# Forgetting attention of a four-layer network: the rows of log gates spread over the partitions by DMA from DRAM instead of by one-hot matmuls

## The chip, the cores and the metric

One Trainium2 chip, one of its cores. The metric is the device time of the whole kernel in microseconds (us), as the median of its runs; below, times inside the program are those of one profiled execution.

## What is computed

The reference runs two blocks, one after the other. The first has two layers on 512 + 256 tokens (differential attention with a gated delta net, then neighbourhood attention). The second has two "hybrid" layers on 528 tokens, 16 learned ones and 512 others; each has eight heads of forgetting attention, four heads of retention, a projection and a feed-forward part. The change is in the forgetting attention:

```python
def fox_attention(q, k, v, logf):
    # logit[t,s] = q_t.k_s/sqrt(Dh) + c[t] - c[s], c = cumsum(log f), s <= t
...
logf = jax.nn.log_sigmoid(flog.astype(jnp.float32) + b_fgate.astype(jnp.float32))
fox_out = fox_attention(fq.reshape(fshape), fk.reshape(fshape), fv.reshape(fshape), logf)
```

A softmax over s is not altered by c[t], which is the same in a whole row of logits. What the kernel has to add is -c[s]: one row of 528 numbers per head, the same on all partitions, since queries lie on the partitions and keys along the free dimension.

## The kernel before, in words

**Arithmetic.** Every product of weights is taken in exact halves: a weight tile arrives by DMA on SP's queue in one of four raw buffers (`top.wraw`), ACT casts its high half (`top.whi`, L457), DVE takes the low half (`top.wlo`, L458), and TensorE does three matmuls for each pair of tiles (L581 and L862).

**Order.** The program is written through a scheduler of tiles. Each piece of work stands in a stream ("L" for projections, "A" for forgetting attention, "B" for retention) with PSUM banks of its own; `later(n)` gives work a lower place, so that it fills gaps of the stream beside it. The order of each engine, which is fixed when the program is built, comes out of that. SBUF for larger tiles is cut into zones (`NZONE`, 24 of them), which are handed out for the whole program, the longest free first.

**A hybrid layer** (`hybrid`, L2192). The five tiles of the first projection give the raw gates and the queries and keys of pairs 0 and 1. `fox_gates` (L1622) makes the log gates, sums them along the tokens and ends with eight rows of 528, times -8, as exact halves `rh`, `rl` (ACT L1666, DVE L1667). Then come `fox(0)`, `fox(1)`, `ret(0)`, `fox(2)`, `ret(1)`, `fox(3)`, the tail, `ret(2)`, `ret(3)` and the projection out. `fox(p)` does the projections of a pair of heads and puts `fox_pair` (L1715) under `later(200)`, so that its small matmuls stand among those of the retention's projection (`retproj.L`, L581).

**A pair.** For each of its two heads, `fox_pair` takes a ring tile `cb` of 128 x 512, and spreads the head's row over 128 partitions: two matmuls (L1729) of a one-hot column of the 8 x 8 identity, broadcast to 128 columns, by the rows, high half and low half, into a PSUM tile `fox.A`, and an ACT copy (L1730) to `cb`. The ring has two tiles. Then, for query tiles 0 and 1, 2, and 3, come q k products (L1742), the causal mask (L1745), the sum with `cb` and its maximum on DVE (L1754), the exponential on ACT (L1757), transposes (L688 by way of a helper) and the product with the values (L1768).

**The tail.** `fox_tail` (L1671) does the last 16 queries of all heads as one tile of 128 rows, in two halves of 272 and 256 keys. Per half there are q k products (L1681), two matmuls with a constant `hselr` that gives rows 16 h to 16 h + 15 the log gates of head h (L1685), an ACT copy (L1686), in the second half a mask (L1688), and the sum and maximum (L1689).

Of the kernel before, what the change touches and what calls it, by code (L numbers as in the profile page):

```python
# [11 lines left out]
F32 = mybir.dt.float32  # L12
# [8 lines left out]
P = 128  # L21
D = 1024
KT = D // P
T = 512
# [9 lines left out]
NZONE = 24  # L34
# [14 lines left out]
# ---------------------------------------------------------------- host layout  # L49

def _fm(w):
    """[K, N] -> [N/128, 128, K]: per column tile, the K tiles side by side."""
    k, n = w.shape
    return np.ascontiguousarray(
        w.reshape(k // P, P, n // P, P).transpose(2, 1, 0, 3)).reshape(n // P, P, k)


def _tm(w):
    """[1024, N] -> [N/256, 2, 128, 1024]: 256-column chunks in two halves of K."""
# [5 lines left out]
def _col(v):  # L65
    """[..., n*128] -> [128, ... * n] (feature on partitions)."""
# [4 lines left out]
def _rows(v):  # L71
    """1-d data repeated on all partitions."""
# [4 lines left out]
def _down(w, groups):  # L77
    """[2816, 1024] -> flat pieces per (hidden group, output tile)."""
# [10 lines left out]
def _headperm(n_heads, dh):  # L89
    """columns of each dh-wide head: even ones first, then odd ones."""  # L90
# [4 lines left out]
# order of the grid's columns in the neighbourhood layer: rolled by 8 columns, column-major  # L95
# [8 lines left out]
def _na_bias(rpb):  # L104
    """[8, 15, 31] -> [8, 128, 3, 256]: bias of each query tile's two key tiles (first, inner, last)."""
# [14 lines left out]
def _const_tables():  # L120
# [7 lines left out]
    # masks added to logits: causal [query, key], and its mirror  # L128
# [4 lines left out]
    hq = np.arange(P) // META  # L133
    t["hsel"] = np.zeros((P, P), f)
    t["hsel"][:8] = np.arange(8)[:, None] == hq[None]
    t["tmask"] = np.where(np.arange(META)[None] <= (a % META)[:, None], 0.0, NEG).astype(f)
    t["mask1"] = ((blk[:, None] == blk[None] + 1) & (blk[:, None] % 2 == 1)).astype(f)
    # rotary tables of the grid positions, even dims first
# [10 lines left out]
    # rotary tables of the second block  # L149
# [5 lines left out]
    # retention decay: [key, query - first key of the tile], key scale folded in  # L155
# [8 lines left out]
def layout(i):  # L164
# [9 lines left out]
    # [l, section, k, 128, 1024]  # L174
    o["ada_w"] = np.ascontiguousarray(g["ada_w"].reshape(2, KT, P, 6, D).transpose(0, 3, 1, 2, 4))
    # the first two sections, by quarters of the columns: [quarter, half of the features, 128, 4 tiles, 256]
# [50 lines left out]
# ---------------------------------------------------------------- kernel  # L227

class K:
    def __init__(self, tc, a, out, ctx):  # L230
# [11 lines left out]
        self.used = np.zeros((NZONE, ZONE // UNIT))     # when a unit was given back; inf: in use  # L242
# [14 lines left out]
    # ------------------------------------------------------------ SBUF: zones of one type, given out in pieces  # L257
    def take(self, n, dtype=F32, top=False, low=False, ring=False, pack=None):
        """n free columns of a zone of the type, or of an empty one: those that have been free for longest."""
# [2078 lines left out]
```

## Time and profile before

| | |
|---|---|
| runs shown (us) | 3464.41, 3473.41, 3473.85; median 3473.41 |
| span of the profiled execution (us) | 3471.1 |
| median less that span (us) | 2.3 |
| mean granted TensorE clock | 0.983 |
| PE busy | 3331.4 us, 96% |
| DVE, ACT, POOL busy | 65%, 41%, 25% |
| DMA | 101 GB/s, SP's queue (q1) 29.9% of 16 engines |

The span runs from the first to the last instruction; a run's time also takes in what lies around it. PE is TensorE's matmuls and PEld its weight loads, which lie beside them. The views with stretches give busy microseconds of each engine in a stretch, and the clock that TensorE was granted there, as a share of full speed (1.00 is 2.4 GHz, 0.50 is 1.2 GHz).

### The profile page before, as it was taken

How to read it: one execution, taken by the hardware profiler on the slowest of the kernel's cores; microseconds unless marked ns; L12 is line 12 of the kernel's file. 1: busy time of each engine (PE TensorE's matmuls, PEld its weight loads, DVE VectorE, ACT ScalarE, POOL GpSimd, SP SyncE). 2: the span in 40 equal slices, each digit the busy share in tenths (PEclk: the TensorE clock that was granted, in tenths of full speed). 3: DMA queues.
4: the chain of work that ended last, by engine and by line, in shares of the span. 5: the costliest groups of instructions: out<-in, count | busy, mean ns of one | idle time of the engine just before them, and what ended most of it. 6: DMA issues, size and time to landing. Idle time of an engine off the chain costs nothing.

```text
span 3471.1 us, 63453 instructions
## 1 busy us (share of the span) xinstructions
PE 3331.4 (96%) x25746; PEld 3071.4 (88%) x25746; DVE 2243.5 (65%) x4401; ACT 1423.0 (41%) x2617; POOL 862.7 (25%) x708
## 2 busy tenths in 40 slices
PE   7999989999999999999999999999999999999998
PEld 6877867799999899998999988899999988889998
DVE  6566766696885655546967844458688543478766
ACT  4355442353444334335433443334344443334434
POOL 0001152053341102111543410005235100033533
PEclk9999999999999999999999999999999999999999
DMA  6112256323335763112233411121333311123232
GB/s 216 42 36 69 81 165 197 125 92 98 104 109 184 275 234 94 63 44 90 72 94 100 128 65 53 49 73 63 98 104 94 121 41 59 34 92 98 88 102 96
DMA packets 124070, 350.52 MB, mean 101 GB/s; under 512 B 27904, under 2 KB 31104, under 8 KB 123776
## 3 DMA queue, kind: packets, MB, share of 16 engines
q1 hardware_dynamic: 116288, 337.17, 29.9%
q10 hardware_dynamic: 7488, 9.29, 0.9%
q8 instruction: 202, 3.31, 0.4%
q14 instruction: 92, 0.75, 0.1%
HBM read 331.73 MB, written 14.68 MB: 100 GB/s over the span
## 4 chain that ended last, share of the span: by engine, by line
PE 54%; DVE 13%; issue 7%; ACT 3%; POOL 1%; DMA 1%; DVEq 0%; ACTq 0%; POOLq 0%; SPq 0%
PE ffn.L L581 20%; PE ffn.L L862 10%; PE retproj.L L581 5%; PE foxproj.L L581 4%; DVE top.wlo L854 4%; PE naproj.L L645 3%; PE outp.L L581 2%; PE fox.A L1742 2%; DVE top.zone L896 1%; ACT top.whi L853 1%; PE fox.Ao L1768 1%; PE ret.B L1825 1%; PE naattn.Ao L1586 1%; PE fox.A L688 1%; PE ada.E L918 1%
## 5 line engine op out<-in xcount | busy, mean ns | idle before, releaser
L457 ACT CAST top.whi<-top.wraw 128x1024 fp32r<-128x1024 f32 (+2 forms) x305 | 294.4, 969 | 543.2 <-PE ffn.L L581 245.2
L458 DVE TENSOR_TENSOR top.wlo<-top.wraw,top.whi 128x1024 fp32r<-128x1024 f32 (+2 forms) x305 | 353.4, 1162 | 232.4 <-ACT top.whi L457 230.8
L862 PE MATMUL ffn.L<-outp.zone,top.whi 128*128 128x256 f32 (+1 forms) x1862 | 407.5, 282 | 8.5 <-ACT top.whi L853 8.5
L862 PEld LDWEIGHTS ffn.L<-outp.zone,top.whi 128*128 128x128 f32 x1862 | 309.1, 189 | 9.3 <-ACT top.whi L853 9.3
L862 PE MATMUL ffn.L<-outp.zone,top.wlo 128*128 128x256 f32 (+1 forms) x1026 | 292.7, 285 | 16.5 <-DVE top.wlo L854 16.1
L581 PE MATMUL ffn.L<-ffn.zone,top.whi 128*128 128x256 f32 (+1 forms) x1460 | 295.9, 283 | 0.0
L854 DVE TENSOR_TENSOR top.wlo<-top.wraw,top.whi 128x1024 fp32r<-128x1024 f32 x152 | 241.9, 1592 | 52.5 <-ACT top.whi L853 52.0
L581 PE MATMUL ffn.L<-outp.zone,top.whi 128*128 128x256 f32 (+1 forms) x1214 | 272.5, 282 | 0.5 <-ACT top.whi L457 0.4
L862 PE MATMUL ffn.L<-norm.zone,top.whi 128*128 128x256 f32 (+1 forms) x1178 | 265.3, 283 | 0.0
L845 POOL TENSOR_TENSOR top.zone<-top.wraw,top.wraw 128x512 f32<-128x512 f32 x76 | 116.6, 1535 | 594.5 <-DMA top.wraw<-in_w_up_dram 494.1
L581 PEld LDWEIGHTS ffn.L<-ffn.zone,top.whi 128*128 128x128 f32 x1460 | 233.4, 189 | 0.6 <-DVE ffn.zone L899 0.4
L862 PE MATMUL ffn.L<-norm.zone,top.wlo 128*128 128x256 f32 (+1 forms) x798 | 227.6, 285 | 5.9 <-DVE top.wlo L854 5.6
L862 PEld LDWEIGHTS ffn.L<-outp.zone,top.wlo 128*128 128x128 f32 x1026 | 193.8, 189 | 23.2 <-DVE top.wlo L854 23.0
L581 PE MATMUL ffn.L<-ffn.zone,top.wlo 128*128 128x256 f32 (+1 forms) x758 | 213.1, 282 | 0.0
L581 PEld LDWEIGHTS ffn.L<-outp.zone,top.whi 128*128 128x128 f32 x1214 | 203.2, 189 | 2.6 <-issue 1.6
L853 ACT CAST top.whi<-top.wraw 128x1024 fp32r<-128x1024 f32 x152 | 158.8, 1045 | 102.1 <-PE ffn.L L581 69.1
L862 PEld LDWEIGHTS ffn.L<-norm.zone,top.whi 128*128 128x128 f32 x1178 | 199.7, 189 | 0.3 <-ACT top.whi L853 0.2
L581 PE MATMUL ffn.L<-gsolve.zone,top.whi 128*128 128x256 f32 x688 | 164.7, 287 | 0.3 <-ACT top.whi L457 0.3
L862 PEld LDWEIGHTS ffn.L<-norm.zone,top.wlo 128*128 128x128 f32 x798 | 151.1, 189 | 8.6 <-DVE top.wlo L854 8.6
L854 DVE TENSOR_TENSOR top.wlo<-top.zone,top.whi 128x1024 fp32r<-128x1024 f32 x76 | 144.6, 1903 | 8.0 <-ACT top.whi L853 8.0
L581 PE MATMUL ffn.L<-outp.zone,top.wlo 128*128 128x256 f32 (+1 forms) x528 | 148.7, 282 | 0.0
L862 PE MATMUL ffn.L<-gsolve.zone,top.whi 128*128 128x256 f32 (+1 forms) x570 | 146.2, 283 | 0.0
(1369 smaller groups left out, 9959.8 us busy)
## 6 DMA issues: line engine op xcount, KB each, us to landing
top.wraw<-in_w_up_dram SPq DMA_DIRECT2D x220, 512.0 KB, 3.5
top.wraw<-in_w_dn_dram SPq DMA_DIRECT2D x89, 448.0 KB, 3.4
top.wraw<-in_w_hy_dram SPq DMA_DIRECT2D x58, 512.0 KB, 3.5
top.zone<-in_ada_w_dram SPq DMA_DIRECT2D x48, 512.0 KB, 5.4
top.wraw<-in_w_dn_dram SPq DMA_DIRECT2D x40, 512.0 KB, 3.7
top.wraw<-in_ada_w_dram SPq DMA_DIRECT2D x32, 512.0 KB, 5.0
top.wraw<-in_w_gdn_dram SPq DMA_DIRECT2D x17, 512.0 KB, 3.5
quads.zone<-in_ada_w_dram SPq DMA_DIRECT2D x16, 512.0 KB, 4.7
```

The costliest lines, as they stand in the source:

```text
L457: nc.scalar.copy(hi[:, :m], raw[:, c:c + m])
L458: nc.vector.tensor_sub(lo[:, :m], raw[:, c:c + m], hi[:, :m].bitcast(F32))
L581: nc.tensor.matmul(ps[:, :n], w[:, wc], x[ks[j]][:, c0:c0 + n], start=a, stop=b)
L645: nc.tensor.matmul(pst[t][:, :256], cols(x, k, t), ww[:, wc], start=a, stop=b)
L688: self.nc.tensor.transpose(dst[:, i * P:i * P + m], s, self.ident[:m, :m])
L845: nc.gpsimd.tensor_sub(s23[:, 512:], rg[:, :512], ru[:, :512])
L853: nc.scalar.copy(wh[:, :m], src)
L854: nc.vector.tensor_sub(wl[:, :m], src, wh[:, :m].bitcast(F32))
L862: nc.tensor.matmul(ps[:, :h], ww[:, wc], xx[k], start=st, stop=sp)
L896: nc.vector.tensor_mul(sg[:, :n], sg[:, :n], su[:, :n])
L918: nc.tensor.matmul(ps[32 * g:32 * g + 32, :256], self.sil[:, k, :], w[:, g * 256:(g + 1) * 256], start=k == 0, stop=k == KT - 1, tile_posi ...
L1742: nc.tensor.matmul(ss[r][:, off[i] + a:off[i] + b], fq[fs, i * P:n], fk[fs, a:b], start=True, stop=b < n)
```

## The change

The rows are kept in DRAM, and each place that needs one reads it with a DMA whose source repeats the row on all partitions.

- `fox_gates`: one plain tile `frow` takes the eight rows from PSUM by ACT alone; a DMA on SP's queue writes it to a DRAM tile `rows` of 8 x 528, which is returned. The two slots of halves and the DVE instructions go.
- `fox_pair`: the two matmuls and the ACT copy of each head become a DMA of a 2 KB row to 128 partitions, 256 KB written. The ring `cb` has four tiles.
- `fox_tail`: the two matmuls and the copy of each half become eight DMAs of one row of 528 to 16 partitions, into a new temporary `ftb`; the mask is added to it once.
- The constants `identr`, `hsel` and `hselr` go, and there are 25 zones.

```diff
-NZONE = 24
+NZONE = 25
...
-        rh, rl = self.rslot("hn", pack=True), self.rslot("hn", pack=True)
+        r = self.slot("frow")
         for p, a, n in ((pr, 0, T), (pq, T, META)):
-            nc.scalar.activation(rh[:8, a:a + n], p[:8, :n], AF.Copy, scale=-8.0)
-            nc.vector.scalar_tensor_tensor(rl[:8, a:a + n], p[:8, :n], -8.0, rh[:8, a:a + n].bitcast(F32),
-                                           ALU.mult, ALU.subtract)
-        return rh, rl
+            nc.scalar.activation(r[:8, a:a + n], p[:8, :n], AF.Copy, scale=-8.0)
+        d = self.tc.dram_tile([8, TB], F32, name=self.nm("rows"))
+        nc.sync.dma_start(d, r[:8, :TB])
+        self.free(r)
+        return d
...
-        e = self.tmp("fte")
+        e, b = self.tmp("fte"), self.tmp("ftb")
...
+        for h in range(FOX_H):
+            nc.sync.dma_start(b[h * META:(h + 1) * META, :TB], rows[h:h + 1, :].to_broadcast([META, TB]))
+        nc.vector.tensor_add(b[:, T:TB], b[:, T:TB], self.tmask)
...
-            pb = self.ps()
-            for j, r in enumerate(rows):
-                nc.tensor.matmul(pb[:, :n], self.hsel[:8, :], r[:8, c0:c0 + n], start=j == 0, stop=j == 1)
-            nc.scalar.copy(e[:, c0:c0 + n], pb[:, :n])
-            if i:
-                nc.vector.tensor_add(e[:, T:TB], e[:, T:TB], self.tmask)
-            nc.vector.tensor_tensor_reduce(out=e[:, c0:c0 + n], in0=ps[:, :n], in1=e[:, c0:c0 + n], scale=0.125,
+            nc.vector.tensor_tensor_reduce(out=e[:, c0:c0 + n], in0=ps[:, :n], in1=b[:, c0:c0 + n], scale=0.125,
...
             cb = self.ring("cb")
-            pb = self.ps()
-            sel = self.identr[:8, 2 * p + r:2 * p + r + 1].to_broadcast([8, P])
-            for j, rw in enumerate(rows):
-                nc.tensor.matmul(pb, sel, rw[:8, 0:T], start=j == 0, stop=j == 1)
-            nc.scalar.copy(cb, pb)
+            nc.sync.dma_start(cb, rows[2 * p + r:2 * p + r + 1, 0:T].to_broadcast([P, T]))
             cbs.append(cb)
...
-    MIX2 = (..., cb=(T, 2), ...)
+    MIX2 = (..., cb=(T, 4), ...)
...
-        self.identr = self.keep([8, 8], "identr", F32R)
-        nc.vector.tensor_copy(self.identr, self.ident[:8, :8])
-        hs = self.const("hsel")
-        self.hsel = self.keep([P, P], "hselr", F32R)
-        nc.vector.tensor_copy(self.hsel, hs)
...
-        self.free(rows)
```

Counted over the whole program, PE has 40 matmuls fewer (32 of 8 x 512, four of 8 x 272, four of 8 x 256), ACT 20 copies fewer, DVE six instructions fewer, and SP 34 DMAs more (two writes of the rows, 16 reads to 128 partitions, 16 reads to 16 partitions).

**SP in the first hybrid layer, where the rows are written and first read.** Before, the weights' DMAs (`w_hy`) stand here alone. Now:

```order
L438 DMA top.wraw_61<-in_w_hy_dram 128x1024 [waits DMAHW4_49,DVE_49]
L1665 DMA foxg.rows_20325<-foxproj.zone_19964 8x528 [waits DMAHW2_49,Activation_49]
L438 DMA top.wraw_62<-in_w_hy_dram 128x1024 [waits DMAHW5_49,DVE_49]
L1721 DMA quads.zone_16326<-foxg.rows_20325 128x512 [waits DMAHW2_49]
L1721 DMA norm.zone_19956<-foxg.rows_20325 128x512 [waits PE_49]
L1721 DMA norm.zone_19956<-foxg.rows_20325 128x512 [waits DMAHW6_49]
L1721 DMA norm.zone_19956<-foxg.rows_20325 128x512 [waits DMAHW7_49]
L438 DMA top.wraw_63<-in_w_hy_dram 128x1024 [waits DMAHW1_49,DMAHW0_49,DVE_49]
L438 DMA top.wraw_64<-in_w_hy_dram 128x1024 [waits DMAHW1_49,DVE_49]
```

The write of the rows waits for ACT, one weight stands between it and the first read, and the four reads of pairs 0 and 1 follow in one piece, ahead of the next two weights.

**PE in the same layer, at pair 0.** `fox.A_20403` and `fox.A_20404` are the scores of the two heads. Before:

```order
L581 MATMUL foxproj.L_20553<-norm.zone_19698,top.wlo_70 128x256
L1729 MATMUL fox.A_20395<-outp.zone_5953,norm.identr_19941 128x512
L1729 MATMUL fox.A_20395<-gsolve.zone_5356,norm.identr_19941 128x512
L1729 MATMUL fox.A_20399<-outp.zone_5953,norm.identr_19941 128x512
L1729 MATMUL fox.A_20399<-gsolve.zone_5356,norm.identr_19941 128x512
L1742 MATMUL fox.A_20403<-foxproj.zone_19961,norm.zone_19956 128x128
```

Now, with `fox.A_20400` and `fox.A_20401` as the two heads:

```order
L578 MATMUL foxproj.L_20550<-norm.zone_19706,top.wlo_70 128x256
L1733 MATMUL fox.A_20400<-foxproj.zone_19962 128x128
L1733 MATMUL fox.A_20401<-foxproj.zone_19962 128x128
L1736 LDWEIGHTS start.identb_103
L1736 MATMUL fox.A_20400<-start.negmb_118,start.identb_103 128x128
```

The four one-hot matmuls are gone, and the heads take turns from the first product.

**PE at pair 2 of the same layer, now.** Before, four one-hot matmuls stood ahead of this among products of the retention's projection, and the mixture below followed with the same shapes.

```order
L578 MATMUL retproj.L_21423<-gsolve.zone_5360,top.whi_67 128x256
L1733 MATMUL fox.A_21209<-foxproj.zone_19962,ret.zone_20965 128x128
L578 MATMUL retproj.L_21423<-norm.zone_19706,top.whi_67 128x256
L1733 MATMUL fox.A_21210<-foxproj.zone_19962,ret.zone_20965 128x128
L578 MATMUL retproj.L_21423<-gsolve.zone_5360,top.wlo_70 128x256
L1736 LDWEIGHTS start.identb_103
```

One q k product still stands between every two products of the projection.

Because there is one zone more, tiles of the whole program are handed other zones, and the order shifts in places that the diff does not touch, most of all in the gated delta net of the first block (some 350 to 700 us after the start): there the copies to and from DRAM of tiles that are set aside (`gprep.spill`, `gproj.spill`) stand up to a few places earlier or later on SP's queue.

## Rows read from the trace of the kernel before

**Rows 1.** The page: the span, and busy time of each engine

```profile
span 3471.1 us, 63453 instructions
PE 3331.4 (96%) x25746; PEld 3071.4 (88%) x25746; DVE 2243.5 (65%) x4401; ACT 1423.0 (41%) x2617; POOL 862.7 (25%) x708
```

**Rows 2.** One line's instructions (L1729): count, ns min/median/max, first and last start

```profile
L1729 PE MATMUL fox.A<-outp.zone,norm.identr x16: 383/440/498, 2060.0 to 2952.7; 8*128 8x512 f32 x16
```

**Rows 3.** PE's timeline at pair 0 of the first hybrid layer: start us, us

```profile
2059.97 0.50 PE L1729 MATMUL fox.A<-outp.zone,norm.identr 8*128 8x512 f32 x1
...
2060.54 0.39 PE L1729 MATMUL fox.A<-outp.zone,norm.identr 8*128 8x512 f32 x1
2060.78 0.38 PE L1729 MATMUL fox.A<-gsolve.zone,norm.identr 8*128 8x512 f32 x1
2061.09 0.49 PE L1742 MATMUL fox.A<-foxproj.zone,norm.zone 64*128 64x128 f32 x2
```

**Rows 4.** PE's timeline at pair 2 of the same layer

```profile
2152.87 0.49 PE L1729 MATMUL fox.A<-outp.zone,norm.identr 8*128 8x512 f32 x1
2153.30 0.39 PE L581 MATMUL retproj.L<-norm.zone,top.wlo 128*128 128x272 f32 x1
2153.62 0.49 PE L1729 MATMUL fox.A<-gsolve.zone,norm.identr 8*128 8x512 f32 x1
...
2154.51 0.38 PE L581 MATMUL retproj.L<-ffn.zone,top.whi 128*128 128x256 f32 x1
```

**Rows 5.** PE's timeline at the first half of that layer's tail

```profile
2255.28 0.39 PE L1685 MATMUL foxt.A<-outp.zone,norm.hselr 8*128 8x272 f32 x1
2255.51 0.28 PE L1685 MATMUL foxt.A<-gsolve.zone,norm.hselr 8*128 8x272 f32 x1
2255.72 0.55 PE L688 MATMUL fox.A<-start.ident,top.zone 128*128 128x128 f32 x3
```

**Rows 6.** Stretches of 5 us: busy us of each engine, granted clock, DMA share, GB/s

```profile
2060.00:2065.00 5.00, 5.00 (x27) 3.78 (x27) 2.70 (x14) 4.43 (x8) 0.00 (x0) 0.90 0.34 93
2065.00:2070.00 5.00, 5.00 (x26) 3.84 (x27) 1.60 (x10) 2.08 (x8) 0.00 (x0) 0.76 0.03 11
2085.00:2090.00 5.00, 5.00 (x43) 3.39 (x41) 0.46 (x2) 3.07 (x7) 0.76 (x1) 1.00 0.21 88
2155.00:2160.00 5.00, 5.00 (x17) 3.33 (x18) 0.07 (x1) 1.51 (x2) 0.76 (x1) 0.61 0.08 34
2160.00:2165.00 5.00, 5.00 (x20) 4.14 (x21) 1.51 (x12) 1.71 (x8) 0.00 (x0) 0.50 0.02 5
...
2225.00:2230.00 5.00, 5.00 (x15) 3.34 (x15) 0.00 (x0) 0.00 (x0) 0.00 (x0) 0.50 0.00 0
2230.00:2235.00 5.00, 5.00 (x24) 4.59 (x24) 2.21 (x13) 1.37 (x6) 0.00 (x0) 0.54 0.00 0
...
2890.00:2895.00 5.00, 5.00 (x20) 4.14 (x20) 1.59 (x12) 1.48 (x7) 0.00 (x0) 0.50 0.01 2
```

**Rows 7.** The page's DMA issues: count, KB each, us to landing

```profile
top.wraw<-in_w_hy_dram SPq DMA_DIRECT2D x58, 512.0 KB, 3.5
...
top.wraw<-in_w_ho_dram SPq DMA_DIRECT2D x32, 256.0 KB, 2.6
...
gbase.gscr<-gprep.zone SPq DMA_DIRECT2D x12, 24.0 KB, 1.9
```

**Rows 8.** Timelines of ACT, SP and DVE around pair 0: start us, us, idle before

```profile
2053.15 0.65 ACT L1666 ACTIVATE outp.zone<-foxg.A 8x512 fp32r<-8x512 f32 x2 [3.33 <-PE foxg.A L1661]
...
2056.29 0.33 SPq L441 DMA_DIRECT2D top.wraw<-in_w_hy_dram  x1
...
2062.68 0.29 DVE L1754 CUSTOM_DVE_ANT_0 top.zone<-fox.A,quads.zone 128x128 f32<-128x128 f32 x1 [0.38 <-PE fox.A L1745]
```

**Rows 9.** Gated delta net, 300 to 700 us: busy us, and POOL's longest wait

```profile
sum 400.00, PE 368.07 PEld 302.19 DVE 261.98 ACT 158.05 POOL 97.07; mean PE 92.02 PEld 75.55 DVE 65.50 ACT 39.51 POOL 24.27
...
POOL top.zone L1410 <- DMA dsetup.zone<-gprep.spill: 15.2, 1, 15.2
```

More of the change, by code (lines that the diff above doesn't have):

```diff
@@ L132, in _const_tables @@
     blk = a // 32
-    hq = np.arange(P) // META
-    t["hsel"] = np.zeros((P, P), f)
-    t["hsel"][:8] = np.arange(8)[:, None] == hq[None]
     t["tmask"] = np.where(np.arange(META)[None] <= (a % META)[:, None], 0.0, NEG).astype(f)
@@ L1865 @@
             dict(L=(512, 3), A=(512, 3), Ao=(512, 2)))
-    MIX2 = (dict(acc=(512, 1), tL=(272, 3), tA=(TB, 6), cb=(T, 2), dec=(TB, 1), vtail=(P, 8), tail=(P, 2), ftl=(P, 1), sL=(8, 10), sA=(48, 12), sB=(32, 10)),
+    MIX2 = (dict(acc=(512, 1), tL=(272, 3), tA=(TB, 6), cb=(T, 4), dec=(TB, 1), vtail=(P, 8), tail=(P, 2), ftl=(P, 1), sL=(8, 10), sA=(48, 12), sB=(32, 10)),
             dict(L=(512, 2), A=(512, 3), Ao=(512, 1), B=(512, 2)))
```

## The prediction

> **What bounds the kernel now.** I read the page's busy times first, then TensorE's instructions at the lines that go, then the granted clock in short stretches, then the DMA queue and the engine that will wait for it. PE is busy 3331.4 of 3471.1 us, 96% of the span, DVE 65%, ACT 41% [rows 1]. So PE's own time sets the end: what is taken from PE's list of instructions shows in the total, and what is taken from ACT or DVE shows only where PE waits for it. In the stretches of the forgetting attention PE is busy 5.00 of 5 us almost throughout [rows 6], so there is no gap in which its one-hot matmuls could have hidden. The same rows show a second thing: beside that full list of work the granted clock is at times near 0.50, the lower of its two levels (1.2 GHz).
>
> **One-hot matmuls (PE).** There are 32 of them, 8 x 512, four for each pair of heads, four pairs, two layers, with a median of 440 ns [rows 2]. A record's duration overlaps the next one, so I take what PE's timeline gives from start to start. At pair 0 the four begin at 2059.97 and the next product begins at 2061.09: 1.12 us [rows 3]. At pair 2 they take 2152.87 to 2153.30 and 2153.62 to 2154.51: 0.43 + 0.89 = 1.32 us [rows 4]. The mean of the two, 1.22 us, by eight pairs is **9.8 us**. Below, the bare step between two of them is 2060.54 to 2060.78, 0.24 us [rows 3], and 32 x 0.24 = 7.7 us; above, 32 x 0.440 = 14.1 us [rows 2]. I take the timeline's value, because it has the weight loads and the changes of shape in it.
>
> **The tail's matmuls (PE).** The two of the first half begin at 2255.28, and the next instruction at 2255.72: 0.44 us [rows 5]. Two halves in two layers make four times that, **1.8 us**. The chain to the tail's maximum gets shorter by matmuls and copy, but PE has other work there, so I count nothing more.
>
> **ACT and DVE.** Twenty ACT copies go, and six DVE instructions. Neither engine sets the end [rows 1]; I cost this at nothing. The cover is PE's queue of projection products; if it were gone, the reduction that follows a copy would come a copy's time earlier for each pair, a gain, not a loss. The kernel's start loses two small casts on DVE and one small load: nothing.
>
> **The write and reads of the rows (SP).** The rows are ready when ACT's two copies end, 2053.15 + 0.65 = 2053.80 [rows 8]. The write to DRAM is 17 KB; the nearest row is a 24 KB write to DRAM, 1.9 us to landing [rows 7], so it is there at about 2055.7. One weight stands on SP between the write and the first read; it was issued at 2056.29 and an issue takes 0.33 us [rows 8], so the first read goes out at about 2056.6. A read of 256 KB lands after 2.6 us and one of 512 KB after 3.5 us [rows 7], so each 256 KB more costs 0.9 us. The first read therefore lands between 2056.6 + 2.6 = 2059.2 and, if it comes wholly behind the weight, 2056.29 + 3.5 + 0.9 = 2060.7; the second 0.9 us later. DVE's first sum was at 2062.68 [rows 8] and, without the four matmuls, can come 1.12 us sooner, at 2061.56. So I cost the wait at **nothing**, with a margin of about one to two microseconds. No row shows one 2 KB row read 128 times; if that read took twice a row's time from DRAM (5.2 us), the first would land near 2061.8 and the second near 2063, a stall of up to 1.5 us in each layer, **0 to 3 us** in all. A gain is excluded here, since nothing waited for ACT's copy but this same sum. The write itself waits for ACT on SP's queue, and behind it stand only weights; the next of them went out at 2056.29, after the rows are ready, so nothing is held up. The two weights behind the four reads are issued 4 x 0.33 = 1.3 us later, which the ring of four raw buffers covers. Reads of pairs 1 to 3 are issued a pair ahead, because the ring has four tiles. In the tail, eight reads stand ahead of the weights of the projection out: 8 x 0.33 = 2.6 us later for a weight that waits behind the whole of two retention heads. The copy of the decay table moves behind one more weight; it is used only after the scores of a retention head: nothing.
>
> **The clock.** After the one-hot matmuls of pairs 0, 2 and 3 the clock falls, though PE is busy 5.00 of 5 us [rows 6]. What that costs is (1 - clock) x 5 us for each stretch: pair 0, 0.10 and 0.24 of five, 1.7 us; pair 2, 0.39 and 0.50, 4.45 us; pair 3, 0.50 and 0.46, 4.8 us [rows 6]; the second layer shows the same at its pair 2, 0.50 [rows 6]. That is 11 us in a layer, 22 us in both. At pair 1, where one-hot matmuls are followed by q k products without the fine mixture with projections, the clock stays at 1.00 [rows 6]. So two things precede each long fall: matmuls that use 8 of 128 rows, and then q k products that use 64, mixed one to one with projections. The change removes the first and keeps the second. For pair 0, with nothing but a short run of q k products left, I expect no fall: **3.4 us** in two layers. For pairs 2 and 3 the bounds are 0 (the mixture alone brings the fall) and 18.5 us (2 x 9.25, no fall at all); of the work at the front of the fall, 1.3 of some 3.2 us from 2152.87 to the fall near 2156 goes, so I take half, **9.2 us**.
>
> The Trainium skill, "TensorE: Matmul & The Clock Gate", section "Why this matters for your kernels", speaks against this term: it ties drops of throughput in mid-kernel to gaps in which TensorE is idle, and asks only that it be kept busy. By that rule the removal of busy matmuls gives nothing back in clock, and the sum would be that of the second rival below. The trace does not agree with it, with a clock of 0.50 in a stretch that is busy 5.00 of 5.
>
> **What the diff does not touch.** One zone more hands other zones to tiles of the whole program, and the gated delta net of the first block gets another order. PE is idle there 400 - 368 = 32 us of 400, spread over many waits [rows 9], and more room can shorten some waits and lengthen others. I take nothing; as bounds, a third of that idle time either way, 10 us.
>
> **Sum.** 9.8 + 1.8 + 3.4 + 9.2 = 24.2 us less. The span 3471.1 becomes 3446.9; the median of the runs shown stands 2.3 us above that span, so the time is 3449 us. A measurement of this kernel can tell about 0.3% from no change, 10.4 us: faster is below 3463.0, slower above 3483.8.
>
> **Rivals.**
> - *The clock stays at full level* through pairs 2 and 3 too. For it: pair 1, which falls nowhere. Against: the mixture that is still there. 11.6 + 22 = 33.6 us less, **3440 us**.
> - *The clock falls as before.* The 1.2 GHz stretches begin while q k products and projections alternate, and that piece of PE's list is kept. Only 11.6 us go, **3462 us**, on the edge of what can be told. This is what the rule cited above comes to as well.
> - *The wait moves to the DMA.* The reads are late, as bounded above, and PE, whose order is fixed, stands before the transposes of pair 0; the idle stretch then takes the clock's gain at pair 0 with it. With the falls kept at pairs 2 and 3 that is 11.6 - 3 = 8.6 us less, **3465 us**; the change would then mostly rename the wait. For it: the one weight in the way and the margin of one to two microseconds. Against: DMA shares of 0.34 and less in these stretches [rows 6].
> - *Slower: the gated delta net waits for a tile that is read back.* With other zones, copies of set-aside tiles stand elsewhere on SP's queue. One such read already kept POOL waiting 15.2 us once [rows 9], with PE fed by other work meanwhile. If three more of that length were to fall where PE has nothing else, 45.6 us would be lost against 24.2 gained: **3495 us**. It decides from 24.2 + 10.4 = 34.6 us of new idle time on PE. Against: PE's 32 us of idle time there are many short waits, and a zone more means fewer tiles set aside in haste.
>
> **How the numbers follow.** Forecast (part of the clock comes back) 0.42, own range 3440 to 3462; clock wholly back 0.15; falls as before 0.23; wait moved to the DMA 0.10; slower by the gated delta net 0.10. Faster: 0.40 of the first, all of the second, 0.12 of the third and 0.03 of the fourth, 0.70. Slower: the last, 0.10. The same: the rest, 0.20. The range goes down to the full clock with 10 us from the gated delta net and the upper bound of the one-hot matmuls, 3440 - 10 - 4.3 = 3426, and up to the late reads with 10 us lost there, 3465 + 10 = 3475; it leaves out the slower case and the edges.
>
> **What would show it.** Right: in the layers' pairs, PE's timeline goes from the last projection to the first q k product with no step between; DVE's first sum at a pair waits for PE and not for a DMA; windows of 5 us after pair 0 show a clock of 1.00, those after pairs 2 and 3 shorter stretches at 0.50. Wrong: a DMA as releaser of DVE's sum or of the transposes; the same stretches at 0.50 as before (second rival); PE's busy time in 300 to 700 us more than 10 us away from 368 (the zones, not the change, then speak in the total).

## The result, and the profile after

The change took 3447.9 us (median of four runs, 3441.28 to 3451.4), the kernel before 3473.63 us beside it. The ratio is 0.9941, with a 95% interval of 0.9924 to 0.9958: 0.6% faster. The forecast was 3449 us, 3426 to 3475. The profiled execution has a span of 3442.9 us against 3471.1.

The page of the change, the span and the engines' busy time, answers to [rows 1]:

```profile
span 3442.9 us, 63375 instructions
PE 3303.7 (96%) x25706; PEld 3051.1 (89%) x25706; DVE 2238.1 (65%) x4395; ACT 1409.4 (41%) x2595; POOL 862.6 (25%) x708
```

PE's busy time fell by 27.7 us and the span by 28.2. To see where, I cut each run at the first product of a hybrid layer's projection (`foxproj.L`) and at the start of its last retention product (`retproj.L`); below, that piece is "the stage". Busy time of PE, PEld, DVE, ACT and POOL in the two stages of the kernel before, then the granted clock, DMA share and GB/s:

```profile
2008.10:2306.10 298.00, 290.07 (x2064) 251.60 (x2063) 130.21 (x403) 107.14 (x233) 21.08 (x28) 0.95 0.16 52
2740.10:3036.00 295.90, 290.14 (x2063) 251.53 (x2062) 129.43 (x404) 106.11 (x230) 20.80 (x28) 0.95 0.17 53
sum 593.90, PE 580.21 PEld 503.12 DVE 259.64 ACT 213.24 POOL 41.88; mean PE 290.11 PEld 251.56 DVE 129.82 ACT 106.62 POOL 20.94
```

The same two stages of the change:

```profile
2011.60:2293.00 281.40, 275.37 (x2044) 241.53 (x2043) 126.54 (x399) 100.97 (x220) 20.58 (x28) 0.98 0.20 64
2725.90:3009.00 283.10, 276.65 (x2043) 243.11 (x2042) 126.19 (x398) 100.92 (x220) 21.46 (x31) 0.98 0.19 62
sum 564.50, PE 552.02 PEld 484.64 DVE 252.73 ACT 201.90 POOL 42.05; mean PE 276.01 PEld 242.32 DVE 126.36 ACT 100.95 POOL 21.02
```

| piece of the span (us) | before | change | difference |
|---|---|---|---|
| up to the first stage | 2008.1 | 2011.6 | +3.5 |
| stage, first hybrid layer | 298.0 | 281.4 | -16.6 |
| between the stages | 434.0 | 432.9 | -1.1 |
| stage, second hybrid layer | 295.9 | 283.1 | -12.8 |
| after | 435.1 | 433.9 | -1.2 |

So the two stages gave 29.4 us, all of the gain and a little more. PE has 20 matmuls fewer in each. Of the 29.4, PE's idle time in the stages (length less busy time) gave 593.9 - 580.2 = 13.7 against 564.5 - 552.0 = 12.5, 1.2 us. The clock's part, as (1 - clock) x 5 us summed over stretches of 5 us, was 13.6 + 13.7 = 27.3 us before and is 5.1 + 6.8 = 11.9 us, 15.4 us less. The remaining 12.8 us is PE's own work, that is, its busy time less the clock's part: 552.9 us before, 540.1 us in the change.

Not all of the clock's part lies in the forgetting attention. In both kernels each stage also has a fall, that is, a stretch at the lower level, 0.50, some 8 to 12 us after its start, behind idle time of PE. Before, in the first layer, the fall at 2019.6 us came right behind this one:

```profile
2019.45 0.49 PE L581 MATMUL foxproj.L<-ffn.zone,ffn.zone 128*128 128x272 f32 x1 [4.53 <-ACT norm.zone L1599]
```

These falls at the start cost 3.4 us before and 5.1 us in the change. The falls at the pairs, with PE busy without a break ahead of them, cost 23.9 us before (3.4 at pair 0 and 20.5 at pairs 2 and 3 of the two layers) and 6.8 us in the change, all of it at pairs 2 and 3. So the pairs gave 17.1 us in this execution, and the starts took 1.7 back.

Stretches of 5 us of the change in the first layer, at pairs 0, 2 and 3, and in the second layer ahead of and in the fall of pair 2 and at pair 3, answer to [rows 6]:

```profile
2060.00:2065.00 5.00, 5.00 (x47) 4.52 (x46) 1.07 (x1) 2.52 (x4) 0.00 (x0) 1.00 0.92 279
2065.00:2070.00 5.00, 5.00 (x31) 3.57 (x29) 3.14 (x21) 3.29 (x11) 0.00 (x0) 1.00 0.39 141
...
2155.00:2160.00 5.00, 5.00 (x24) 4.37 (x25) 1.51 (x12) 1.86 (x8) 0.00 (x0) 0.67 0.00 2
...
2215.00:2220.00 5.00, 5.00 (x25) 3.42 (x24) 1.32 (x3) 0.18 (x1) 0.76 (x1) 1.00 0.24 93
...
2865.00:2870.00 5.00, 5.00 (x28) 3.54 (x26) 1.72 (x4) 0.08 (x1) 1.75 (x2) 1.00 0.30 105
2870.00:2875.00 5.00, 5.00 (x23) 4.59 (x23) 1.65 (x13) 2.10 (x9) 0.00 (x0) 0.51 0.00 2
...
2935.00:2940.00 5.00, 5.00 (x29) 4.83 (x28) 3.13 (x17) 2.91 (x9) 0.27 (x1) 0.66 0.00 0
```

Pair 0 has no fall any more, pair 3 of the first layer has none, and pair 2 keeps one, shorter in the first layer (0.67 where 0.61 and 0.50 followed each other). In the second layer pairs 2 and 3 both keep a shorter one. PE's timeline at pair 0 answers to [rows 3]:

```profile
2062.59 0.28 PE L578 MATMUL foxproj.L<-norm.zone,top.wlo 128*128 128x256 f32 x1
2062.80 0.49 PE L1733 MATMUL fox.A<-foxproj.zone 64*128 64x128 f32 x4
2063.23 0.28 PE L1736 MATMUL fox.A<-start.negmb,start.identb 128*128 128x128 bf16 x2
```

From the last projection to the first q k product there is 0.21 us, and nothing in between. The rows' way through DRAM, on the timelines of SP and DVE, answers to [rows 8]:

```profile
2056.68 0.34 SPq L1665 DMA_DIRECT2D foxg.rows<-foxproj.zone  x1
2059.14 0.35 SPq L438 DMA_DIRECT2D top.wraw<-in_w_hy_dram  x1
2059.54 0.41 SPq L1721 DMA_DIRECT2D quads.zone<-foxg.rows  x1
2060.01 1.37 SPq L1721 DMA_DIRECT2D norm.zone<-foxg.rows  x3
...
2063.93 1.23 DVE L455 TENSOR_TENSOR top.wlo<-top.wraw,top.whi 128x1024 fp32r<-128x1024 f32 x1 [4.81 <-ACT top.whi L454]
2065.07 0.28 DVE L1745 CUSTOM_DVE_ANT_0 top.zone<-fox.A,quads.zone 128x128 f32<-128x128 f32 x1
```

And what waited for the reads, with the time from issue to landing, from the line's own view:

```profile
who waited for it (us, times):
  DVE top.zone L1745: 0.2, 1
...
DMA to landing us min/median/max: 3.2/4.3/6.0
```

The reads take 4.3 us, not 2.6, and yet DVE waited for one of them once, 0.2 us: DVE's half of a weight (L455), 1.23 us long, stood ahead of the first sum and hid them. The first read landed at 2064.13, and PE had projections to do until its first transpose of the pair at 2066.87.

### The profile page after: what moved, and what is told of

The parts are those of the page before. It is cut to its first block, busy times and chain, and to the rows that moved or that the text cites. A ratio compares the mean times of both kernels' runs of the same rounds, so it can differ in the third digit from the quotient of the medians.

```text
span 3442.9 us, 63375 instructions
## 1 busy us (share of the span) xinstructions
PE 3303.7 (96%) x25706; PEld 3051.1 (89%) x25706; DVE 2238.1 (65%) x4395; ACT 1409.4 (41%) x2595; POOL 862.6 (25%) x708
## 4 chain that ended last, share of the span: by engine, by line
PE 60%; DVE 14%; issue 12%; ACT 3%; POOL 2%; DMA 2%; DVEq 0%; POOLq 0%; ACTq 0%; SPq 0%
PE ffn.L L578 21%; PE ffn.L L859 12%; PE retproj.L L578 5%; PE outp.L L578 4%; PE foxproj.L L578 4%; DVE top.wlo L851 3%; PE gproj.L L578 2%; PE fox.A L1733 1%; DVE top.zone L893 1%; ACT top.whi L850 1%; PE fox.Ao L1759 1%; PE ret.B L1816 1%; PE fox.A L685 1%; PE naproj.L L642 1%; PE ada.E L915 1%
## 5 line engine op out<-in xcount | busy, mean ns | idle before, releaser
L455 DVE TENSOR_TENSOR top.wlo<-top.wraw,top.whi 128x1024 fp32r<-128x1024 f32 (+2 forms) x305 | 352.4, 1159 | 244.6 <-ACT top.whi L454 239.8
L859 PE MATMUL ffn.L<-outp.zone,top.whi 128*128 128x256 f32 (+1 forms) x1900 | 421.3, 284 | 13.4 <-ACT top.whi L850 13.4
L578 PE MATMUL ffn.L<-ffn.zone,top.whi 128*128 128x256 f32 (+1 forms) x1742 | 373.9, 284 | 0.4 <-ACT top.whi L454 0.3
L578 PE MATMUL ffn.L<-outp.zone,top.whi 128*128 128x256 f32 (+1 forms) x1552 | 344.2, 282 | 0.5 <-ACT top.whi L454 0.5
L859 PEld LDWEIGHTS ffn.L<-outp.zone,top.whi 128*128 128x128 f32 x1900 | 318.8, 190 | 14.2 <-ACT top.whi L850 14.2
L578 PEld LDWEIGHTS ffn.L<-ffn.zone,top.whi 128*128 128x128 f32 x1742 | 287.6, 189 | 12.3 <-issue 9.1
L859 PE MATMUL ffn.L<-outp.zone,top.wlo 128*128 128x256 f32 (+1 forms) x988 | 283.5, 287 | 15.0 <-DVE top.wlo L851 14.8
L859 PE MATMUL ffn.L<-norm.zone,top.whi 128*128 128x256 f32 (+1 forms) x1368 | 289.6, 283 | 0.4 <-ACT top.whi L850 0.4
L578 PE MATMUL ffn.L<-ffn.zone,top.wlo 128*128 128x256 f32 (+1 forms) x1000 | 282.9, 283 | 1.4 <-DVE top.wlo L455 1.4
L578 PEld LDWEIGHTS ffn.L<-outp.zone,top.whi 128*128 128x128 f32 x1552 | 259.6, 189 | 4.4 <-issue 2.9
L859 PEld LDWEIGHTS ffn.L<-norm.zone,top.whi 128*128 128x128 f32 x1368 | 224.6, 189 | 1.0 <-ACT top.whi L850 1.0
L859 PE MATMUL ffn.L<-norm.zone,top.wlo 128*128 128x256 f32 (+1 forms) x646 | 184.4, 285 | 10.7 <-DVE top.wlo L851 10.7
L578 PEld LDWEIGHTS ffn.L<-ffn.zone,top.wlo 128*128 128x128 f32 x1000 | 189.1, 189 | 2.1 <-DVE top.wlo L455 1.6
L845 POOL TENSOR_TENSOR quads.zone<-top.wraw,top.zone 128x512 f32<-128x512 f32 x76 | 148.0, 1947 | 21.3 <-DVE outp.zone L814 9.6
```

The lines of the kernel that those rows point to most:

```text
L455: nc.vector.tensor_sub(lo[:, :m], raw[:, c:c + m], hi[:, :m].bitcast(F32))
L578: nc.tensor.matmul(ps[:, :n], w[:, wc], x[ks[j]][:, c0:c0 + n], start=a, stop=b)
L845: nc.gpsimd.tensor_sub(s4, rg[:, 512:], s23[:, :512])
L859: nc.tensor.matmul(ps[:, :h], ww[:, wc], xx[k], start=st, stop=sp)
```

## Experiments

**Theory A:** the gain is TensorE's list of work, made shorter, and the clock, which falls less where fewer matmuls with few rows stand in the stage. **Rivals:** B, the other handing out of zones brings the gain; C, what cost were the copies and the PSUM tiles, not the matmuls; and for the clock, that the mixture of small and large products brings the falls whatever its rows.

**The zones alone, in the kernel before.**

```diff
-NZONE = 24
+NZONE = 25
```

> The kernel before, with 25 zones instead of 24 and nothing else. Theory A (the gain comes from TensorE's removed matmuls and from the clock in the forgetting attention): 3468 to 3478 us, as before; the stretches of 1.2 GHz in the forgetting attention stay at some 24 us a layer. Theory B (the other handing out of zones gives a good part of the gain, through the gated delta net): 3455 to 3463 us.

Measured 3484.25 us, ratio 1.0047 (1.0029 to 1.0065): 0.5% slower, some 16 us, which neither theory had. The two stages took 293.6 + 295.1 us, 5.2 less than before; the first stage began at 2022.8 us, 14.7 later than before. B falls: the zones bring no gain.

**The change without the zone.** Four ring tiles for the rows don't fit in 24 zones, so the ring has two.

```diff
-NZONE = 25
+NZONE = 24
...
-cb=(T, 4)
+cb=(T, 2)
```

> The change with 24 zones and a ring of two tiles for the spread rows instead of four (four do not fit in 24 zones). Theory A: 3443 to 3455 us, as the change; with two tiles the reads of the next pair are issued only when the pair before has been summed, and still land ahead of their use. Theory B: 3460 us or more, since the zones are those of before. If the ring of four is what hides the reads, DVE waits for reads at pairs 1 to 3 and the time is 3455 or more too, but then with a DMA as the releaser of DVE's sum.

Measured 3444.68 us, ratio 0.9941 (0.9923 to 0.9958), the same as the change; stages 286.3 and 282.3 us. No DMA stands among the releasers of DVE's sum, so two tiles are enough. In the profiled execution the first stage began at 2001.7 us, ten earlier than in the change, and what follows took ten longer. In the profiled runs of this study the first stage began at 2008.1, 2012.7 and 2013.9 us in the three forms of the kernel before with 24 zones, and between 2005.7 and 2022.2 us in the nine forms of the change with 25, whose text is the same up to there. The spread among programs that are alike is larger than the difference, so a time of the zone can't be read from there. One piece of it can. In the profiled execution of every kernel with 25 zones PE stands once for 8.2 to 8.3 us in the last feed-forward part of the first block, waiting for a weight's high half, with a clock fall of 10.2 us beside it; the kernels with 24 zones don't stand there. The change with 24 zones stands for as long in a feed-forward part behind the first stage instead:

```profile
2395.66 0.59 PE L859 MATMUL ffn.L<-outp.zone,top.whi 128*128 128x264 f32 x1 [8.69 <-ACT top.whi L850]
```

Of the ten microseconds that what follows took longer, 3.7 lie in that piece, 4.9 in the first stage. So the zone brings no gain, here or in the kernel before, and its whole cost in the change stays **open**.

**Matmuls of the one-hot kind put back, and the same with 128 rows.** Two matmuls per head, of the shape of the one-hot ones, on other data; nobody reads the result. The first takes 8 rows, the second 128 (`[:, ...]` for `[:8, ...]`); the order of every engine is the same in the two.

```diff
             cb = self.ring("cb")
+            pb = self.ps()
+            for j in range(2):
+                nc.tensor.matmul(pb, self.dum[0][:8, 0:P], self.dum[1][:8, 0:T], start=j == 0, stop=j == 1)
```

> The change, with two matmuls of 8 x 512 per head put back where the one-hot matmuls stood; they multiply other data and nobody reads their result, and there is no ACT copy. Theory A: 9.8 us of matmuls come back and with them most of the stretches of 1.2 GHz in the forgetting attention (14 us of them now, 48 us before): 3465 to 3475 us. Rival C (the copies and the waits for PSUM were what cost, not the matmuls): 3445 to 3452 us. If the matmuls cost their own time but the clock does not follow them: about 3458 us.

> As the run with 8-row matmuls put back, in the same order on every engine, but each takes 128 rows (128 x 512) instead of 8. If the clock falls because the array is fed few rows, the stretches of 1.2 GHz are as short as with the change and the time is about 3458 us (9.8 us of matmul time alone), some 10 us below the run with 8 rows. If the rows do not matter, only time and order, it equals the run with 8 rows within 5 us.

Measured 3457.8 us, ratio 0.9979 (0.9968 to 0.9989), with 8 rows, and 3447.49 us, 0.9948 (0.9933 to 0.9963), with 128. The stages with 8 rows:

```profile
2005.70:2293.40 287.70, 281.76 (x2059) 245.48 (x2058) 127.19 (x399) 101.28 (x220) 19.52 (x28) 0.96 0.20 62
2725.80:3014.60 288.80, 282.44 (x2059) 246.44 (x2058) 126.84 (x398) 100.12 (x219) 20.11 (x31) 0.96 0.20 60
```

The stages with 128 rows:

```profile
2011.80:2294.40 282.60, 278.33 (x2060) 245.06 (x2059) 127.14 (x399) 101.32 (x220) 20.64 (x28) 0.97 0.20 63
2730.10:3012.50 282.40, 275.74 (x2059) 242.69 (x2058) 126.84 (x398) 100.25 (x219) 20.11 (x31) 0.98 0.19 62
```

One number alone is different, the rows, and the stages are 576.5 and 565.0 us long, 11.5 apart, with a clock of 0.96 against 0.97 and 0.98. At the pairs the falls cost 17.1 us with 8 rows, more than in either execution of the change (6.8 here, 13.7 in the run again below), and 10.2 with 128, between these two. The mean granted clock of all executions says the same: 0.984 in 12 with 8 rows, 0.987 in five with 128, which is about 12 us of such a kernel. So matmuls of 8 rows cost more than their time, and most of that is clock: PE's own work is 542.0 and 540.4 us. Rival C is not borne out, since the PSUM tiles are back in both runs and the one with 128 rows is as fast as the change; the copies alone were not run.

Both came out about 10 us under what I expected. The 8-row time by itself, 3457.8, fits the third case of its expectation, in which the clock does not follow; it is the clock in the traces and the run with 128 rows that speak against that case. With 128 rows, 32 matmuls more left the stages where they are in the change (564.5), and I had priced them at 9.8. Part of this is the order that the scheduler made with the extra PSUM tile: it has fewer steps between products of 64 or 8 rows and products of 128. Counted along PE's instructions, a stage has 108 such changes of rows before, 90 in the change, 92 with 8 rows put back and 80 with 128, beside 28 around products of 16 and 32 rows that are the same in all. At the 0.2 us that a change costs in the mixture (below), 20 fewer in the two stages are 4 us; the rest is open.

**The change once more**, on the chip of the next three runs.

> The change itself once more, beside the three other runs on the same chip: a ratio to the kernel before of 0.992 to 0.996, and a stage from the first projection of a hybrid layer to its last retention projection of 281 to 284 us in each layer (296 to 298 before).

Measured 3452.38 us, ratio 0.995 (0.9936 to 0.9964); stages 282.7 and 283.5 us. This is the same program with the same order, and two things can be compared. PE's own work in the stages is 540.4 us, against 540.1 in the first execution (540.7 with 24 zones), so what the change takes from PE's work is steady. The falls at the pairs cost 13.7 us here and 6.8 in the first execution: all four, at pairs 2 and 3 of both layers, are there, for 6.8 us each. At pair 3 of the first layer, where the first execution had 1.00:

```profile
2225.00:2230.00 5.00, 5.00 (x24) 4.81 (x25) 2.67 (x15) 2.91 (x9) 0.00 (x0) 0.50 0.00 0
```

So what the clock gives back differs by 7 us from one execution of the change to the next.

**q k products over 128 rows.**

```diff
-nc.tensor.matmul(ss[r][:, off[i] + a:off[i] + b], fq[fs, i * P:n], fk[fs, a:b],
+nc.tensor.matmul(ss[r][:, off[i] + a:off[i] + b], fq[:, i * P:n], fk[:, a:b],
```

> The change, with the q k products of the forgetting attention taken over all 128 rows (both heads' features together, so that the scores are not those of one head) instead of 64; the order of every engine is the same. Theory A (stretches with few rows in use are what the falls follow): the 14 us in the two stages that remain at 1.2 GHz go, some 7 us or more below the change, the more so if a switch between 64 and 128 rows costs time of its own. Rival (the mixture of small and large products itself, whatever its rows): the same as the change within 3 us.

The scores then sum both heads' features, so this kernel leaves out the separation of the heads; it is for its time alone. Measured 3421.4 us, ratio 0.9865 (0.9853 to 0.9878): 31 us below the change on the same chip, with every engine's order unaltered.

```profile
2013.70:2281.70 268.00, 262.34 (x2044) 237.87 (x2043) 126.67 (x399) 100.92 (x220) 20.60 (x28) 0.99 0.21 67
2714.90:2981.60 266.70, 260.44 (x2044) 236.10 (x2043) 126.31 (x399) 99.88 (x219) 21.14 (x31) 1.00 0.21 65
```

The clock is back: there is no fall at the pairs any more, only one at the start of the first stage. Beside it each stage lost some 10 us of PE's work. The reason stands in PE's timeline at pair 2. The change, with 64 rows, at full clock:

```profile
2151.78 0.49 PE L1733 MATMUL fox.A<-foxproj.zone,ret.zone 64*128 64x128 f32 x2
2152.20 0.39 PE L578 MATMUL retproj.L<-norm.zone,top.whi 128*128 128x256 f32 x1
2152.51 0.48 PE L1733 MATMUL fox.A<-foxproj.zone,ret.zone 64*128 64x128 f32 x2
```

The same place with 128 rows:

```profile
2149.57 0.38 PE L1733 MATMUL fox.A<-foxproj.zone,ret.zone 128*128 128x128 f32 x2
2149.71 0.36 PE L578 MATMUL retproj.L<-norm.zone,top.whi 128*128 128x256 f32 x1
2149.91 0.39 PE L1733 MATMUL fox.A<-foxproj.zone,ret.zone 128*128 128x128 f32 x2
```

A turn of the mixture, one group of q k products and one projection, takes 2152.51 - 2151.78 = 0.73 us with 64 rows and 2149.91 - 2149.57 = 0.34 us with 128, for the same columns: 0.39 us for a change of rows and back, about 0.2 us each. The rival, that the mixture brings the falls whatever its rows, is out.

**The pairs' work not put lower**, so that q k products stand together.

```diff
-            with self.later(200):
+            with self.later(0):
                 self.fox_pair(p, fq, fk, v[0], rows, lhs, f)
```

> The change, with the work of a pair no longer put 200 places lower in the scheduler, so that its q k products stand together and not one to one among the projections. Theory A (mixed products of 64 rows cost a switch each and bring the falls): pairs 2 and 3 lose their falls and some 0.2 us for each of some 20 switches a pair, 10 to 20 us below the change, if waits for DVE and ACT do not come in their place. Rival (the mixture is what covers the softmax): PE waits for DVE and ACT at the transposes and the time is the same or longer than the change.

Measured 3427.48 us, ratio 0.9886 (0.9874 to 0.9899), 25 us below the change, more than I had said. The stages took 268.9 us each, the clock was 1.00 in both, and the changes of rows are 62 in a stage. PE's own work fell by some 15 us. PE's idle time stayed (6.0 and 6.8 us), so the mixture was not needed to cover the softmax.

**Each read issued twice.**

```diff
+            nc.sync.dma_start(cb, rows[2 * p + r:2 * p + r + 1, 0:T].to_broadcast([P, T]))
             nc.sync.dma_start(cb, rows[2 * p + r:2 * p + r + 1, 0:T].to_broadcast([P, T]))
```

> The change, with each read of a spread row to 128 partitions issued twice into the same tile. If the reads are wholly covered, except for the few tenths of a microsecond at pair 0: 0 to 2 us more than the change, with DVE's first sum at pair 0 waiting for the DMA. If the DMA's time is on the path: 3 us or more for each of the 16 reads that is not covered.

Measured 3449.27 us, ratio 0.9948 (0.9934 to 0.9963), the same as the change (0.995). The edit also moved PE's order: a stage has 84 changes of rows instead of 90, and PE's own work is some 8 us less than in the change, so equal totals do not show that the reads are free. What ended DVE's waits ahead of its sums:

```profile
its engine sat idle before it (us, times) until:
  PE fox.A L1737: 76.4, 22
  DMA quads.zone<-foxg.rows: 4.2, 1
  DMA ffn.zone<-foxg.rows: 3.8, 1
```

At pair 0 of both layers DVE now waited some 4 us for the read, and PE's idle time in the stages is 6.7 and 9.2 us, where the change run beside it has 4.0 and 5.2. The stages took 281.9 and 284.7 us, 0.4 us more in sum. The second read of the first head landed at 2076.51, 4.8 us after the first, and DVE waited 4.2 us for it. So the reads are covered as they are, and at pair 0 the cover ends within about 1 us; at the other pairs no DMA stands among the waits ahead of the sums even with each read doubled.

**The kernel before with 128 rows in its q k products**, the same edit as above, one-hot matmuls kept; and **the kernel before with the pairs' work not put lower**.

> The kernel before, one-hot matmuls and all, with its q k products over all 128 rows (both heads' features together) and nothing else; the order of every engine is that of the kernel before. If the q k products of 64 rows are needed for the falls and the one-hot matmuls only lengthen the stretch of few rows: the 27 us a layer at 1.2 GHz shrink to under 10, and with the cheaper switches the ratio to the kernel before is 0.985 to 0.991. If the eight-row matmuls bring the falls by themselves: some 15 to 20 us a layer stay at 1.2 GHz and the ratio is 0.990 to 0.996.

> The kernel before with the work of a pair not put 200 places lower, one-hot matmuls kept. If switches between few and many rows, one-hot or q k, are the price: stretches at 1.2 GHz of under 10 us a layer, ratio 0.987 to 0.993, so that the change's own part beside this order is only its 12 us of matmul time. If the one-hot matmuls' falls stay: ratio 0.993 to 0.998.

The first took 3430.08 us, ratio 0.9891 (0.9873 to 0.9909):

```profile
2012.70:2290.80 278.10, 270.12 (x2063) 242.85 (x2062) 130.16 (x403) 106.70 (x232) 21.06 (x28) 0.99 0.18 56
2725.50:3001.60 276.10, 269.19 (x2063) 241.59 (x2063) 129.74 (x404) 105.90 (x230) 19.77 (x29) 0.99 0.18 56
```

With the one-hot matmuls all there, the clock is 0.99, and the pairs have no fall at all (23.9 us before); the falls that are left stand at the starts of the stages. So the one-hot matmuls do not bring the falls by themselves: they lengthen stretches which the q k products of 64 rows make. The second took 3443.68 us, ratio 0.9924 (0.991 to 0.9937), stages of 280.2 and 280.9 us at 0.99 and 0.98, with one fall at a pair, 1.7 us. So without the mixture the products of 64 rows bring hardly a fall. Set against the runs with the same edit on the change, these give the change's own worth beside that edit: 554.2 - 534.7 = 19.5 us with 128 rows, 561.1 - 537.8 = 23.3 us unmixed, where I had expected 12. Of these PE's own work is 13.1 and 10.1 us, the clock 3.4 and 8.5, nearly all of it at the starts of the stages, and PE's idle time the rest.

**A version that is faster than both kernels.** The scores stay those of one head if the queries of each head have a tile of 128 rows with zeros in the other head's rows.

```diff
+        z = self.slot("fz", n=T)
+        nc.gpsimd.memset(z[0:64, :T], 0.0)
+        nc.gpsimd.tensor_copy(z[64:128, :T], fq[64:128, :T])
+        nc.gpsimd.memset(fq[64:128, :T], 0.0)
+        qz = (fq, z)
...
-nc.tensor.matmul(ss[r][:, off[i] + a:off[i] + b], fq[fs, i * P:n], fk[fs, a:b],
+nc.tensor.matmul(ss[r][:, off[i] + a:off[i] + b], qz[r][:, i * P:n], fk[:, a:b],
```

> The change, with the queries of each head kept in a tile of 128 rows whose other head's rows are zero, so that q k products use 128 rows and give the scores of one head; GpSimd does the clearing and the copy, one more tile for a pair. As the run that took the products over both heads if GpSimd's three instructions for a pair are hidden: ratio 0.985 to 0.990; if the products wait for them at pair 0 and 1, up to 4 us for a pair, 0.990 to 0.994.

> The same with the work of a pair not put 200 places lower. If the two do the same thing in two ways (no switch between row counts in the mixture): 0.984 to 0.989, no better than either by more than 3 us. If each takes away something of its own: 0.980 to 0.984.

Measured 3421.71 us, ratio 0.9861 (0.9846 to 0.9876), and with the pairs' work not put lower besides 3421.74 us, 0.9866 (0.9851 to 0.988). The stages of the first:

```profile
2019.10:2285.00 265.90, 260.62 (x2043) 236.17 (x2042) 128.41 (x400) 100.56 (x219) 27.20 (x40) 1.00 0.21 67
2717.70:2986.50 268.80, 263.10 (x2044) 239.22 (x2043) 127.52 (x399) 99.48 (x218) 28.63 (x40) 0.99 0.20 65
```

GpSimd's 12 instructions more in a layer are hidden: the stages are as long in sum as with the heads not separated (534.7 us). The two ways give the same time, which fits that they take away the same thing: the changes of rows between q k products and projections. The first is 1.4% below the kernel before, where the change is 0.5 to 0.6% below.

## Why the prediction was right

- **PE sets the end, and what leaves its list shows in the total.** It did: busy time 27.7 us less, span 28.2 us less.
- **Matmuls, 9.8 + 1.8 = 11.6 us.** Measured 12.8 us of PE's work without the clock, and 12.2 to 12.8 over three profiled executions (two of the change, one with 24 zones). I read 0.43 us for a one-hot matmul between projections [rows 4] against 0.24 us among its own kind [rows 3] and called the surplus weight loads and shapes. The bare steps and the tail are 7.7 + 1.8 us; the other 3.3 us, put down to the changes of rows, of which a stage has 18 fewer, are 0.09 us each. The pair of runs with 8 and 128 rows, 12 changes apart in a stage and 1.6 us of work in all, says 0.07. Both are estimates, and less than the 0.2 us of the 64-row products in the mixture; why, was not taken apart.
- **ACT and DVE at nothing.** Right; 20 copies less, and PE's idle time in the stages moved by 1.2 us.
- **The write and the reads at nothing, 0 to 3 us.** Right in the sum, wrong in two of its terms. The read lands after 4.3 us (median), not 2.6; one row read on 128 partitions is dearer than the weight rows it was priced by. It went out 2.9 us after the write of the rows, where I had 2.8. What saved it I had not named: a weight's half stands ahead of the sum on DVE until about 2065.1, with the read issued at 2059.54.
- **The clock at pair 0, 3.4 us.** Right: 1.00 in the stretches where 0.90 and 0.76 stood [rows 6], and no fall at pair 0 in the other layer or in the run again.
- **The clock at pairs 2 and 3, 9.2 us, half of 18.5.** The falls there cost 20.5 us before, a little more than I had read from the stretches. The change gave back 13.7 us of them in its first execution, 6.8 in the second, and 12.0 with 24 zones. So half is about right, and no execution by itself can tell it better; the halving itself, argued from the length of what goes, is not shown. The mechanism behind it held: these falls follow stretches of matmuls with few rows among products of 128, of which the change takes one kind away and leaves the other. The rival by which falls need idle time fell, since PE was busy 5.00 of 5 us ahead of and beside a clock of 0.51, and since 128 rows in place of 8, in the same order, shortened the falls. The Trainium skill, "TensorE: Matmul & The Clock Gate", section "Why this matters for your kernels", names idle gaps as what to avoid; by the falls at the pairs that is not enough, while the traces agree with it elsewhere: all other falls in the kernel before come behind idle time of PE.
- **What the diff does not touch, at nothing.** The span up to the first stage is 3.5 us longer, within the spread that this piece shows. The bounds of 10 us either way were too narrow: the zone alone made the kernel before some 16 us slower. In the gated delta net PE was busy 374.9 us of 400 against 368.1 [rows 9], a gain of 6.8 us; it was lost again in the feed-forward part of the first block, where PE stood once for 8.30 us:

```profile
1688.22 0.58 PE L859 MATMUL ffn.L<-outp.zone,top.whi 128*128 128x256 f32 x1 [8.30 <-ACT top.whi L850]
```

All nine forms of the change with 25 zones have this wait, and the kernel before has it when it is given 25. The slower rival, a gated delta net that waits for tiles read back, did not come.
- **The total.** 24.2 us less was forecast, and 25.7 came. That it is so near is in part luck: in the run again the same program was 16.7 us below the kernel before, which is inside the range too. There the mean granted clock of all executions rose from 0.9845 to 0.9857 only, about 4 us over the whole kernel, so most of that gain is PE's work, and the 12.6 us of clock in the forecast are not steady.

The miss that mattered more than any term was one of view. I took the q k products of 64 rows as given, and the largest gain of this stage, some 31 us in all, lay there, in the rows that I quoted.

## What to carry to other kernels

A matmul with few rows cost three times here: its columns, a change of rows before and after it when it stands among products of 128 rows, and, where many of these follow each other, the clock. So spread small tables by DMA when a DMA has a few microseconds to land, and pad a contraction of 64 rows with zeros to 128 before trying to order it better. Read steps from start to start at full clock, with and without the neighbour of another shape; a stage's granted clock below 1.00 beside a full PE is a sign to look for such places.

## What the runs showed of the hardware that was not expected

- Products of 64 rows by turns with products of 128 took 0.73 us a turn, and 0.34 us with 128 in both, at the full clock.
- With PE busy without a break, the clock fell at the pairs. That cost 23.9 us in two layers with one-hot matmuls and q k products of 64 rows mixed among projections, and 6.8 to 13.7 us without the first. With q k products of 128 rows there was no such fall, whether the one-hot matmuls were there or not. Unmixed, products of 64 rows had no fall either without one-hot matmuls, and one that cost 1.7 us with them. Whether the few rows do that or the slow steps between them was not taken apart.
- A DMA that reads one row of 2 KB on 128 partitions landed after 4.3 us (3.2 to 6.0, the longest where four were issued in a piece), a weight of the same 256 KB after 2.6 us [rows 7]; reads of a row to 16 partitions landed after 1.8 us.
- One execution and the next of the same program differ by some 11 us (the change run again: 3444.58 to 3455.87), and the first stage's beginning by up to 16.5 among nine programs that are alike up to there, so parts of this size were read from the stage and not from the total. In the two profiled executions of the change PE's own work in the stages agrees within half a microsecond, and the clock's part does not.
